# Hybrid encoder block on one core: source order for the first stage's ScalarE and VectorE, and a last norm through rows of sums, a root and a reciprocal

## Chip, cores and metric

The kernel runs on one core of a Trainium2 chip. The metric is the device time of one execution in microseconds (us), the median of several runs.

## What is computed

One encoder layer for two token streams (512 prompt tokens, 1024 sample tokens, width 1024, all float32): a norm, one input projection, differential attention beside a recurrent branch (RG-LRU), an output projection with residual, a second norm, a SwiGLU FFN with residual, and a final norm.

```python
def rmsnorm(x, g):
    xf = x.astype(jnp.float32)
    y = xf * lax.rsqrt(jnp.mean(xf * xf, axis=-1, keepdims=True) + NORM_EPS)
    return (y * g.astype(jnp.float32)).astype(x.dtype)

def encoder_layer(x, ...):
    h = rmsnorm(x, norm_mix)
    q, k, v, xr, gate = jnp.split(h @ w_in, [...], axis=-1)
    ...
    x = x + jnp.concatenate([o, y_lru], axis=-1) @ w_out
    h2 = rmsnorm(x, norm_ffn)
    return x + (jax.nn.silu(h2 @ w_gate) * (h2 @ w_up)) @ w_down
...
    return rmsnorm(x, norm_final)
```

The two places that the change touches are the first `rmsnorm` with the first columns of `h @ w_in` for the prompt, and the final `rmsnorm` for the prompt's last 256 tokens.

## The kernel before, in words

Tokens are held in three blocks of 512 (block 0 the prompt, 1 and 2 the sample), features on the 128 partitions, so a block is eight chunks of 128 x 512. A float32 operand is split into a high part `h` (a rounding to float32r, a cast on ScalarE) and a low part `l` (the rest, a subtraction on VectorE), and every product is three matmuls, h·h, l·h and h·l (`mm3`, L213 to L215).

The instructions are not queued as the source lists them: the tile framework sets the order on each engine from its own estimate of when operands come, and every engine then runs its list strictly in order. Side work (attention, the recurrence, loading the next block) is recorded beside the projection by `advance`, a table of numbers (A1, A2, ...) saying how much of it per step.

The first stage (L856 to L863). `load_block(0, ...)` (L290 on) asks for the block's four pages `xc` (512 KB each, L314) on SyncE's DMA queue, and between the first page and the others for the first weight tile (`fetch(1)`, L191 to L202: DMA `wr`, cast `wh` L200, subtraction `wl` L201). Per chunk it makes `xh` (ScalarE, scaled by the norm's gain, L326) and `xl` (VectorE, L327). The norm's factor is one number per token; it is worked out beside the projection: the squares of the eight chunks (L307, added up by L309), sums over partitions by TensorE (`ss`, L279), a Newton root in twelve small VectorE instructions (L281, L248 to L253), diagonal matrices `dg` (L261) which TensorE turns into a row spread over all partitions (`bc`, L262), and a ScalarE copy of it, `rms` (L339). A projected tile is evicted by multiplying it with that row (`ev`, L375). The projection has three PSUM banks (`pm`), so a fourth tile can't start before the first tile's `ev`. `constants()` (L146) follows: ScalarE makes four scaled copies of each half of a distance table (`d`, L152, from the load L149), which go to DRAM (L153); `lv` and a chain of small VectorE instructions (`tmp`) make scalars that attention needs. Attention of the prompt's first head loads its keys, values (`vr`) and queries back from DRAM, transposes the values on TensorE (`pt`, L514) and makes scores (`sc`, L582 and L583).

The end (L1190 on). The FFN's second product for the prompt's upper output half runs in two token halves, T0 and T1; `finish(0, T0)` (L1094) runs beside T1's matmuls, and after the last matmul come, with nothing beside them: the residual adds (L1079), squares (L1088) and their sum (L1090), the same norm chain for 256 tokens (L279, L281, L248 to L253, L261, L262), a copy of the row (L1103, for GpSimd, which scales two of the eight chunks), the scaling (L1109), and four output DMAs.

Of the kernel before, what the change touches and what calls it, by code (L numbers as in the profile page):

```python
# [11 lines left out]
F32 = mybir.dt.float32  # L12
F32R = mybir.dt.float32r
I32 = mybir.dt.int32
F16 = mybir.dt.float16
AF = mybir.ActivationFunctionType
# [4 lines left out]
P = 128  # L21
D = 1024
KC = D // P
# [7 lines left out]
EPS = 1e-6  # L31
LAM_INIT = 0.2
HALF = (P, BLK)
# [14 lines left out]
YV, YF, YL, YT = 1.0, 1.5, 3.0, 1.5  # L48
GRP, LB, FINE = 1, 5, 4
# [27 lines left out]
def drain(gen):  # L77
    for _ in gen:
        pass


def build(tc, io, es):
    nc = tc.nc
    V, A, T = nc.vector, nc.scalar, nc.tensor
# [4 lines left out]
    cp = pool(es, "const")  # L89
# [3 lines left out]
    rings = {}  # L93
# [17 lines left out]
    def bank(name, tag):  # L111
        return banks[tag].tile([P, BLK], F32, name=name, tag=tag)
# [15 lines left out]
    onesq = cp.tile([P, P], F32, name="onesq")  # L128
# [2 lines left out]

    warm = cp.tile([P, 1], F32, name="warm")
    A.activation(warm, ones, AF.Exp)
    neglam = cp.tile([P, 1], F32, name="neglam")
    subg = cp.tile([P, 1], F32, name="subg")
    hb = cp.tile([P, 16], F32, name="hb")
# [3 lines left out]
    def split(h, l, src, eng=V):  # L140
        A.copy(h, src)  # L141
        eng.tensor_tensor(l, src, h.bitcast(F32), ALU.subtract)  # L142
# [46 lines left out]


    plan, ahead = [], []  # L191

    def fetch(n):
        while plan and len(ahead) < n:
            key = plan.pop(0)
            r = rings["raw"]([P, KC, P], "wr")
            nc.sync.dma_start(r, io[key[0]][key[1]].rearrange("p (k m) -> p k m", k=KC))
            h = rings["w"]([P, KC, P], "wh", F32R)
            l = rings["w"]([P, KC, P], "wl", F32R)
            A.copy(h, r)  # L200
            V.tensor_tensor(l, r, h.bitcast(F32), ALU.subtract)  # L201
            ahead.append((key, (h, l)))  # L202
# [53 lines left out]
    def bcast_cols(tag, r, c0, who="m", n=4):  # L256

        bc = bank("bc", tag)
        for i in range(n):
            dg = small(P, "dg")  # L260
            V.tensor_scalar(dg, ident, r[:, c0 + i:c0 + i + 1], None, ALU.mult)  # L261
            T.matmul(bc[:, i * P:(i + 1) * P], lhsT=onesq, rhs=dg, start=True, stop=True)  # L262
        return bc[:, 0:n * P]
# [11 lines left out]
    def inv_rms_cols(tag, acc, n=4):  # L275

        ss = bank("ss", tag)
        for i in range(n):
            T.matmul(ss[:, i:i + 1], lhsT=acc[:, i * P:(i + 1) * P], rhs=ones, start=True, stop=True)  # L279
        ve = small(n, f"ve{n}")  # L280
        V.tensor_scalar(ve, ss[:, 0:n], 1.0 / D, EPS, ALU.mult, ALU.add)  # L281
        return rsqrt_cols(ve, n)
# [15 lines left out]
    def load_block(b, other=None, xring="raw"):  # L298

        h, l = acts[b] = Block(f"xh{b}", F32R), Block(f"xl{b}", F32R)  # L300
        acc = rings["mh"](HALF, "sqa")
        pages = []

        def square(c):
            r = pages[c // 2][:, c % 2]
            sq = rings["mh"](HALF, "sq") if c else acc
            A.activation(sq, r, AF.Square)  # L307
            if c:
                V.tensor_tensor(acc, acc, sq, ALU.add)  # L309

        def load():
            i = len(pages)
            pages.append(rings[xring]([P, 2, BLK], "xc"))
            nc.sync.dma_start(pages[i], chunks(io["xt"][b], 2 * i))  # L314

        for c in range(KC):
            if c == 0 and other is not None:
                for i in range(4):
                    load()
                    if i == 0:  # L320
                        other()
            elif c % 2 == 0 and other is None:
                load()
            r = pages[c // 2][:, c % 2]
            g = par[:, C_MIX + c:C_MIX + c + 1]
            A.activation(h[c], r, AF.Copy, scale=g)  # L326
            V.scalar_tensor_tensor(l[c], r, g, h[c].bitcast(F32), ALU.mult, ALU.subtract)  # L327
            if b:
                square(c)
            yield 2.0  # L330
        if b == 0:
            for c in range(KC):
                square(c)
        r = inv_rms_cols("lru", acc)
        if b:
            yield YL
        bc = bcast_cols("lru", r, 0)
        rows[b] = rings["rows"](HALF, f"rms{b}")
        A.copy(rows[b], bc)  # L339
        yield 2.0  # L340
# [7 lines left out]
    IN_P = qkv_tiles(0, 1, 2, 3) + lru_tiles(0, 1, 2, 3)  # L348
    IN_S = sum((lru_tiles(i - 4) if i > 3 else qkv_tiles(i) for i in ORDER), [])

    def proj(s, blocks, tiles, ready):

        first = len(blocks) + GRP
        n = len(blocks) * BLK
        xr = None
        for t0 in [0] + list(range(first, len(tiles))):
            group = tiles[t0:t0 + (1 if t0 else first)]
            w, dst = {}, {}
            for m in group:
                w[m] = load_w("w_in", m)  # L360
                if m >= 16:
                    dst[m] = gt = rings["lru"]([P, n], "gt")
                elif m >= 12:
                    xr = rings["xr"]([P, SEQ_S + 32], f"xr{s}")
                    V.memset(xr[:, 0:2], 0.0)
                    V.memset(xr[:, n + 2:n + 3], 0.0)
                    dst[m] = xr[:, 2:n + 2]

            def scaled(pm, m, b):
                o = slice(b * BLK, (b + 1) * BLK)  # L370
                if m in dst:
                    V.tensor_tensor(dst[m][:, o], pm, rows[blocks[b]], ALU.mult)
                else:
                    ev = rings["mh"](HALF, "ev")
                    V.tensor_tensor(ev, pm, rows[blocks[b]], ALU.mult)  # L375
                    nc.scalar.dma_start(qkv[s][m][:, o], ev)

            late = []
            for b, blk in enumerate(blocks):
                for m in group:  # L380
                    pm = bank("pm", "mm")
                    dense(pm, w[m], acts[blk])
                    if blk in rows:
                        scaled(pm, m, b)
                    else:
                        late.append((pm, m, b))
                    yield 5.1
            for args in late:
                scaled(*args)
            done[s].update(group)  # L390
            if group[-1] >= 16:
                ready.append((group[-1] - 16, xr, gt))
# [402 lines left out]
    ALL, T0, T1 = slice(0, BLK), slice(0, BLK // 2), slice(BLK // 2, BLK)  # L795
# [25 lines left out]
    ready = {"p": [], "s": []}  # L821
# [12 lines left out]
    n = (B1 + B2 + 3 + GRP) // 2  # L834
# [18 lines left out]
    for _ in range(WARM):  # L853
        T.matmul(spare[:, 0:P], lhsT=onesq, rhs=onesq, start=True, stop=True)

    lb = load_block(0, lambda: fetch(1), "main")  # L856
    for _ in range(KC):
        next(lb)
    p = proj("p", [0], IN_P, ready["p"])
    for _ in range(1 + GRP):  # L860
        next(p)
    drain(lb)
    constants()  # L863
    advance(p, 92.0, (att_p, A1, 0.0, 1.0), (scan, A2, 0.6, 1.0), (load_block(1), 20.0, A3, 1.0))

    lb = load_block(2)
    for _ in range(LB):
        next(lb)
    p = proj("s", [1, 2], IN_S, ready["s"])
# [14 lines left out]
    bc = inv_rms("pv", sums)  # L884
# [129 lines left out]
    def x_chunk(b, m, tok):  # L1014
        return xs[b][m // 2][:, m % 2, tok]
# [59 lines left out]
    def add(b, ms, acc, tok=ALL, square=False, last=False):  # L1075

        for m, a in zip(ms, acc):
            y = x_chunk(b, m, tok)
            V.scalar_tensor_tensor(y, a, 0.5, y, ALU.mult, ALU.add)  # L1079
            if square:  # L1080
                add_square(b, m, tok)
            if last and m in POOLED:
                A.mul(y, y, par[:, C_FIN + m:C_FIN + m + 1])

    def add_square(b, m, tok):
        key = b, tok.start
        sq = rings["xh" if key in sums else "sums"](HALF, "sqd")[:, 0:tok.stop - tok.start]
        A.activation(sq, x_chunk(b, m, tok), AF.Square)  # L1088
        if key in sums:
            V.tensor_tensor(sums[key], sums[key], sq, ALU.add)  # L1090
        else:
            sums[key] = sq

    def finish(b, tok, tag, last=False):  # L1094

        n = (tok.stop - tok.start) // P
        r = inv_rms_cols(tag, sums[b, tok.start], n)
        yield YF
        bc = bcast_cols(tag, r, 0, n=n)
        yield 1.0  # L1100
        if last:
            row = rings["xh"](HALF, "bcs")[:, tok]
            A.copy(row, bc)  # L1103
        for c in range(KC):
            y = x_chunk(b, c, tok)
            if last and c in POOLED:
                nc.gpsimd.tensor_tensor(y, y, row, ALU.mult)
            else:
                V.scalar_tensor_tensor(y, y, par[:, C_FIN + c:C_FIN + c + 1], bc, ALU.mult, ALU.mult)  # L1109
            if c % 2:  # L1110
                (nc.sync if c % 4 == 1 else nc.scalar).dma_start(chunks(io["out"][b], c - 1)[:, :, tok], xs[b][c // 2][:, :, tok])
            yield 1.0
# [121 lines left out]
```

## Time and profile before

| what | value |
|---|---|
| median of 3 runs | 1765.14 us (1763.05 to 1765.33) |
| the profiled execution's own time | 1766.5 us |
| its span, first to last instruction | 1764.6 us |
| TensorE busy, its mean granted clock | 98% of the span, 0.993 |
| VectorE, ScalarE, GpSimd busy | 75%, 47%, 0% |

The span is what the trace's rows lie in; 1.9 us of the profiled execution are outside it. Busy time of TensorE is modelled (a matmul's row is longer than the distance to the next one), so what is read from it is where it stood idle, and for whom. Rows give the start from the span's start and a duration in us; "L213" is a line of the kernel.

### The profile page before, as it was taken

How to read it: one execution, taken by the hardware profiler on the slowest of the kernel's cores; microseconds unless marked ns; L12 is line 12 of the kernel's file. 1: busy time of each engine (PE TensorE's matmuls, PEld its weight loads, DVE VectorE, ACT ScalarE, POOL GpSimd, SP SyncE). 2: the span in 40 equal slices, each digit the busy share in tenths (PEclk: the TensorE clock that was granted, in tenths of full speed). 3: DMA queues.
4: the chain of work that ended last, by engine and by line, in shares of the span. 5: the costliest groups of instructions: out<-in, count | busy, mean ns of one | idle time of the engine just before them, and what ended most of it. 6: DMA issues, size and time to landing. Idle time of an engine off the chain costs nothing.

```text
span 1764.6 us, 22706 instructions
## 1 busy us (share of the span) xinstructions
PE 1731.0 (98%) x8316; PEld 1432.0 (81%) x8316; DVE 1317.0 (75%) x2291; ACT 830.7 (47%) x1327; POOL 1.6 (0%) x6
## 2 busy tenths in 40 slices
PE   8998999999999999999999989999999999999997
PEld 7787877878878888888878878888888888888897
DVE  6779878778678777787453897777777777987784
ACT  6568657664455554555342443332223334445451
POOL 0000000000000000000000000000000000000000
PEclk9999999999999999999999999999999999999998
DMA  8532423244383322221364643222323229743261
GB/s 295 185 122 95 155 90 127 71 156 155 103 231 119 114 72 96 84 84 66 125 227 125 191 152 111 101 101 92 107 104 123 92 88 321 264 127 98 96 198 54
DMA packets 103870, 234.56 MB, mean 133 GB/s; under 512 B 12112, under 2 KB 21072, under 8 KB 103760
## 3 DMA queue, kind: packets, MB, share of 16 engines
q1 hardware_dynamic: 75456, 180.85, 32.4%
q10 hardware_dynamic: 28304, 52.28, 7.8%
q8 instruction: 65, 1.06, 0.3%
q14 instruction: 45, 0.37, 0.1%
HBM read 175.80 MB, written 57.28 MB: 132 GB/s over the span
## 4 chain that ended last, share of the span: by engine, by line
PE 88%; DVE 5%; ACT 3%; DMA 3%; issue 1%; SPq 0%; DVEq 0%; ACTq 0%
PE pm L213 5%; PE pm L214 5%; PE pm L215 5%; PE gu L213 4%; PE gu L215 4%; PE gu L214 4%; PE acc L213 4%; PE acc L215 4%; PE acc L214 4%; PE y L213 3%; PE y L215 3%; PE y L214 3%; PE z L215 2%; PE z L213 2%; PE z L214 2%; PE x L215 2%
## 5 line engine op out<-in xcount | busy, mean ns | idle before, releaser
L213 PE MATMUL pm<-xh,wh 128*128 128x512 f32 x480 | 191.0, 398 | 6.0 <-ACT wh L200 3.3
L214 PE MATMUL pm<-xl,wh 128*128 128x512 f32 x480 | 190.0, 396 | 0.8 <-DVE xl L327 0.8
L215 PE MATMUL pm<-xh,wl 128*128 128x512 f32 x480 | 189.7, 396 | 0.0
L200 ACT CAST wh<-wr 128x1024 fp32r<-128x1024 f32 x100 | 105.1, 1051 | 148.5 <-PE gu L214 61.2
L213 PE MATMUL gu<-yh,wh 128*128 128x512 f32 x352 | 142.0, 403 | 0.9 <-DVE ev L375 0.9
L213 PE MATMUL acc<-hp,ws 128*128 128x512 f32 (+1 forms) x396 | 140.5, 355 | 0.0
L215 PE MATMUL acc<-hp,ws 128*128 128x512 f32 (+1 forms) x396 | 140.3, 354 | 0.0
L214 PE MATMUL acc<-hp,ws 128*128 128x512 f32 (+1 forms) x396 | 140.1, 354 | 0.0
L215 PE MATMUL gu<-yh,wl 128*128 128x512 f32 x352 | 139.0, 395 | 0.0
L214 PE MATMUL gu<-yl,wh 128*128 128x512 f32 x352 | 138.6, 394 | 0.0
L201 DVE TENSOR_TENSOR wl<-wr,wh 128x1024 fp32r<-128x1024 f32 x100 | 122.2, 1222 | 17.5 <-ACT wh L200 16.7
L588 ACT ACTIVATE pb<-pb,mn 128x1024 f32<-128x1024 f32 (+1 forms) x96 | 97.0, 1010 | 73.9 <-DVE mn L585 73.8
L585 DVE CUSTOM_DVE_ANT_0 pb<-sc,tab 128x1024 f32<-128x1024 f32 (+1 forms) x96 | 100.1, 1043 | 34.2 <-PE sc L583 32.9
L710 ACT CAST ws<-s 128x512 fp32r<-128x512 f32 x88 | 54.8, 624 | 126.2 <-PE x L215 47.5
L213 PEld LDWEIGHTS pm<-xh,wh 128*128 128x128 f32 x480 | 91.3, 190 | 24.6 <-ACT wh L200 3.5
L214 PEld LDWEIGHTS pm<-xl,wh 128*128 128x128 f32 x480 | 91.3, 190 | 19.4 <-DVE xl L327 1.1
L215 PEld LDWEIGHTS pm<-xh,wl 128*128 128x128 f32 x480 | 91.0, 190 | 19.1 <-DVE wl L201 0.7
L141 ACT CAST hp<-hr 128x512 fp32r<-128x512 f32 (+1 forms) x143 | 77.8, 552 | 56.2 <-PE acc L215 24.4
L142 DVE TENSOR_TENSOR hp<-hr,hp 128x512 fp32r<-128x512 f32 (+1 forms) x143 | 85.3, 608 | 24.8 <-ACT hp L141 21.3
L710 ACT CAST ws<-wr 128x512 fp32r<-128x512 f32 x66 | 41.2, 624 | 102.5 <-PE z L215 43.8
L215 PEld LDWEIGHTS acc<-hp,ws 128*128 128x128 f32 x396 | 74.9, 189 | 10.4
L213 PEld LDWEIGHTS acc<-hp,ws 128*128 128x128 f32 x396 | 74.9, 189 | 10.3
(269 smaller groups left out, 4301.2 us busy)
## 6 DMA issues: line engine op xcount, KB each, us to landing
wr<-w_gate SPq DMA_DIRECT2D x44, 512.0 KB, 3.5
wr<-w_up SPq DMA_DIRECT2D x44, 512.0 KB, 3.5
wr<-w_in SPq DMA_DIRECT2D x40, 512.0 KB, 4.1
hr<-hs SPq DMA_DIRECT2D x77, 256.0 KB, 2.7
hs<-t ACTq DMA_DIRECT2D x44, 256.0 KB, 2.0
hs<-ht ACTq DMA_DIRECT2D x33, 256.0 KB, 2.9
wr<-w_out SPq DMA_DIRECT2D x16, 512.0 KB, 3.6
xc<-xt SPq DMA_DIRECT2D x12, 512.0 KB, 4.0
```

What stands on the lines that cost most here:

```text
L141: A.copy(h, src)
L142: eng.tensor_tensor(l, src, h.bitcast(F32), ALU.subtract)
L200: A.copy(h, r)
L201: V.tensor_tensor(l, r, h.bitcast(F32), ALU.subtract)
L213: T.matmul(out, lhsT=wh, rhs=ah, start=first, stop=False, skip_group_check=more)
L214: T.matmul(out, lhsT=wh, rhs=al, start=False, stop=False, skip_group_check=more)
L215: T.matmul(out, lhsT=wl, rhs=ah, start=False, stop=last, skip_group_check=more)
L585: V.tensor_tensor_reduce(out=pp[m], in0=sc, in1=tab[:, 896 - q0:896 - q0 + n], scale=-0.125, scalar=3e38, op0=ALU.add, op1=ALU.min, accum_ ...
L588: A.activation(pp[m], pp[m], AF.Exp, scale=-1.0, bias=mn, accum_out=zz)
L710: A.copy(h[:, 0], src)
```

## The change

Two places. In the first stage ScalarE and VectorE keep the order of the source (`manual_schedule`), which is rewritten: the first weight tile is loaded and split in two halves that alternate with the first pages and chunks, the second weight is fetched behind the chunks, then four squares, the third weight, four squares. In the last norm (`finish(..., last=True)`) the squares of the last two chunks are not added to the sum: TensorE takes the sum and the two squares as right operands under a matrix of ones, which gives the sum already as a row in all partitions; ScalarE takes the root, VectorE the reciprocal, and ScalarE copies it. A dummy root in the norm of T0 brings the table of the root in ahead.

```diff
+    eps = cp.tile([P, 1], F32, name="eps")
+    V.memset(eps, EPS)
...
+    def first_halves():
+        key = plan.pop(0)
+        r = rings["raw"]([P, KC, P], "wr")
+        h = rings["w"]([P, KC, P], "wh", F32R)
+        l = rings["w"]([P, KC, P], "wl", F32R)
+        src = io[key[0]][key[1]].rearrange("p (k m) -> p k m", k=KC)
+        halves = [slice(0, KC // 2), slice(KC // 2, KC)]
+        for o in halves:
+            nc.sync.dma_start(r[:, o], src[:, o])
+            yield
+        for o in halves:
+            split(h[:, o], l[:, o], r[:, o])
+            yield
+        ahead.append((key, (h, l)))
+        yield
...
                 for i in range(4):
                     load()
-                    if i == 0:
-                        other()
-            elif c % 2 == 0 and other is None:
+                    if i < 2:
+                        next(other)
+            elif c in (1, 2, 3) and other is not None:
+                next(other)
+            if c % 2 == 0 and other is None:
                 load()
...
             for c in range(KC):
                 square(c)
+                if c == 3:
+                    yield 0.0
...
-    lb = load_block(0, lambda: fetch(1), "main")
-    for _ in range(KC):
+    p = proj("p", [0], IN_P, ready["p"])
+    with tc.manual_schedule(engines={mybir.EngineType.Activation, mybir.EngineType.DVE}):
+        lb = load_block(0, first_halves(), "main")
+        for _ in range(KC):
+            next(lb)
+
+        fetch(2)
         next(lb)
-    p = proj("p", [0], IN_P, ready["p"])
-    for _ in range(1 + GRP):
-        next(p)
-    drain(lb)
+        fetch(3)
+        drain(lb)
+        for _ in range(1 + GRP):
+            next(p)
     constants()
...
             if square:
-                add_square(b, m, tok)
+                add_square(b, m, tok, last and m >= KC - 2)
+        for m in ms:
             if last and m in POOLED:
+                y = x_chunk(b, m, tok)
                 A.mul(y, y, par[:, C_FIN + m:C_FIN + m + 1])
...
+        if apart:
+            sq = rings["xh"](HALF, "sqd")[:, 0:tok.stop - tok.start]
+            A.activation(sq, x_chunk(b, m, tok), AF.Square)
+            if not isinstance(sums[key], list):
+                sums[key] = [sums[key]]
+            sums[key].append(sq)
+            return
...
+        w = tok.stop - tok.start
+        if last:
+            ss, bc = bank("ss", tag)[:, 0:w], bank("rb", tag)[:, 0:w]
+            for k, a in enumerate(sums[b, tok.start]):
+                T.matmul(ss, lhsT=onesq, rhs=a, start=k == 0, stop=k == len(sums[b, tok.start]) - 1)
+            root = rings["xh"](HALF, "root")[:, 0:w]
+            A.activation(root, ss, AF.Sqrt, scale=1.0 / D, bias=eps)
+            V.reciprocal(bc, root)
+            row = rings["xh"](HALF, "bcs")[:, 0:w]
+            A.copy(row, bc)
+        else:
+            r = inv_rms_cols(tag, sums[b, tok.start], w // P)
+            if tok is T0:
+                A.activation(warm, r[:, 0:1], AF.Sqrt)
+            yield YF
+            bc = bcast_cols(tag, r, 0, n=w // P)
```

The order moves on every engine. First, ScalarE at the start of the program; before, from its first square to the second weight:

```order
L307 ACTIVATE sqa<-xc 128x512
L307 ACTIVATE sq<-xc 128x512
L200 CAST wh<-wr 128x1024
L326 ACTIVATE xh_292<-xc,par 128x512 x2
L326 ACTIVATE xh_293<-xc,par 128x512 x2
L326 ACTIVATE xh_294<-xc,par 128x512 x2
L326 ACTIVATE xh_295<-xc,par 128x512 x2
L200 CAST wh<-wr 128x1024
L307 ACTIVATE sq<-xc 128x512 x2
```

and now (VectorE's `xl` and `wl` stand in the same order):

```order
L347 ACTIVATE xh_296<-xc,par 128x512
L143 CAST wh<-wr 128x512
L347 ACTIVATE xh_296<-xc,par 128x512
L143 CAST wh<-wr 128x512
L347 ACTIVATE xh_297<-xc,par 128x512 x2
L347 ACTIVATE xh_298<-xc,par 128x512 x2
L347 ACTIVATE xh_299<-xc,par 128x512 x2
L219 CAST wh<-wr 128x1024
L326 ACTIVATE sqa<-xc 128x512
L326 ACTIVATE sq<-xc 128x512 x3
```

The two squares ahead of the first cast are gone, and the first weight's casts stand as halves between the first chunks.

Second, ScalarE around the copy of the norm's row, `rms`; before (`gh` is the recurrence's gate weight, `xh` by now the next block's):

```order
L152 ACTIVATE d_467<-d_456 128x960
L200 CAST wh<-wr 128x1024
L326 ACTIVATE xh_558<-xc,par 128x512 x2
L141 CAST gh<-gr 128x512
L200 CAST wh<-wr 128x1024
L339 COPY rms_454<-bc 128x512
L152 ACTIVATE d_472<-d_470 128x960
L152 ACTIVATE d_475<-d_470 128x960
```

and now:

```order
L154 ACTIVATE d_481<-d_470 128x960
L347 ACTIVATE xh_566<-xc,par 128x512 x2
L143 CAST gh<-gr 128x512
L154 ACTIVATE d_486<-d_484 128x960
L154 ACTIVATE d_489<-d_484 128x960
L362 COPY rms_405<-bc 128x512
L219 CAST wh<-wr 128x1024
L154 ACTIVATE d_492<-d_484 128x960
```

Two pieces of the distance table's second half (`d_486`, `d_489`) now stand ahead of the row's copy, and a weight's cast, the fourth weight's, right behind it. On VectorE the first `ev` stands behind that weight's `wl`, as it stood behind a later weight's before.

Third, TensorE at the transposes of the first head's values, `pt`; before:

```order
L213 MATMUL pm<-xh_293,wh 128x512
L214 MATMUL pm<-xl_297,wh 128x512
L514 MATMUL pt<-ident,vr 128x128 x4
L215 MATMUL pm<-xh_293,wl 128x512
L213 MATMUL pm<-xh_294,wh 128x512
```

and now:

```order
L232 MATMUL pm<-xh_299,wh 128x512
L233 MATMUL pm<-xl_303,wh 128x512
L537 MATMUL pt<-ident,vr 128x128 x4
L234 MATMUL pm<-xh_299,wl 128x512
L232 MATMUL pm<-xh_299,wh 128x512
```

Counted from the first matmul of the fourth tile, 59 matmuls stood ahead of `pt` before and 44 do now.

## Rows read from the trace of the kernel before

**Rows 1.** The page, busy time by engine, whole span.

```profile
PE 1731.0 (98%) x8316; PEld 1432.0 (81%) x8316; DVE 1317.0 (75%) x2291; ACT 830.7 (47%) x1327; POOL 1.6 (0%) x6
```

**Rows 2.** The timeline of TensorE: start, us, what, and idle time before, by releaser.

```profile
29.96 0.50 PE L213 MATMUL pm<-xh,wh 128*128 128x512 f32 x1 [1.40 <-DVE ev L375]
...
46.90 0.50 PE L582 MATMUL sc<-kt,qh 128*128 128x512 f32 x1 [1.17 <-ACT qh L141]
...
48.91 0.80 PE L583 MATMUL sc<-kt,ql 128*128 128x512 f32 x1 [0.81 <-DVE ql L142]
...
175.51 0.80 PE L213 MATMUL pm<-xh,wh 128*128 128x512 f32 x1 [3.27 <-ACT wh L200]
```

**Rows 3.** Windows: busy by engine in a stretch, PEclk, DMA share, GB/s.

```profile
30.00:45.70 15.70, 15.70 (x70) 12.65 (x70) 9.30 (x34) 7.33 (x12) 0.00 (x0) 1.00 0.93 297
...
48.90:52.30 3.40, 3.39 (x8) 2.72 (x9) 1.97 (x4) 1.75 (x3) 0.00 (x0) 0.52 0.41 164
...
178.00:180.00 2.00, 2.00 (x6) 1.61 (x5) 1.97 (x2) 2.00 (x4) 0.00 (x0) 0.50 0.75 240
```

**Rows 4.** The timelines of ScalarE and VectorE, first 15 us.

```profile
6.10 1.05 ACT L200 CAST wh<-wr 128x1024 fp32r<-128x1024 f32 x1 [0.23 <-DMA wr<-w_in]
7.05 5.02 ACT L326 ACTIVATE xh<-xc,par 128x512 fp32r<-128x512 f32 x8
...
8.32 5.38 DVE L327 SCALAR_TENSOR_TENSOR xl<-xc,par,xh 128x512 fp32r<-128x512 f32 x8
13.62 1.22 DVE L201 TENSOR_TENSOR wl<-wr,wh 128x1024 fp32r<-128x1024 f32 x1
```

**Rows 5.** DMA issues at 17.40, 22.61 and 38.86 us: KB, us to landing.

```profile
xc<-xt SPq DMA_DIRECT2D x1, 512.0 KB, 3.6
...
d<-dist SPq DMA_DIRECT2D x1, 480.0 KB, 5.7
...
vr<-qkvp SPq DMA_DIRECT2D x1, 256.0 KB, 4.4
```

**Rows 6.** The timelines of TensorE, VectorE and ScalarE, 18 to 34 us.

```profile
18.55 3.67 ACT L152 ACTIVATE d<-d 128x960 f16<-128x960 f32 x4
...
22.51 0.16 DVE L281 TENSOR_SCALAR ve<-ss 128x4 f32<-128x4 f32 x1 [1.21 <-PE ss L279]
...
27.84 0.71 PE L262 MATMUL bc<-dg,onesq 128*128 128x128 f32 x4 [0.28 <-DVE dg L261]
...
28.59 0.59 ACT L339 COPY rms<-bc 128x512 f32<-128x512 f32 x1 [1.05 <-PE bc L262]
...
29.21 1.89 DVE L375 TENSOR_TENSOR ev<-pm,rms 128x512 f32<-128x512 f32 x3
...
33.22 0.33 ACTq L376 DMA_DIRECT2D qkvp<-ev  x1
```

**Rows 7.** The timeline of the last norm, all engines, from its last sums on.

```profile
1751.76 1.47 DVE L1090 TENSOR_TENSOR sqd<-sqd 128x256 f32<-128x256 f32 x3
...
1753.94 0.16 DVE L281 TENSOR_SCALAR ve<-ss 128x2 f32<-128x2 f32 x1 [0.70 <-PE ss L279]
...
1756.73 1.20 PE L262 MATMUL bc<-dg,onesq 128*128 128x128 f32 x4 [2.83 <-DVE dg L261]
1757.96 0.37 ACT L1103 COPY bcs<-bc 128x256 f32<-128x256 f32 x1 [5.67 <-PE bc L262]
```

**Rows 8.** VectorE's groups by shape: busy us, mean ns of one, idle before.

```profile
L523 DVE RECIPROCAL cf<-z 128x1 f32<-128x1 f32 x48 | 7.7, 161 | 16.6 <-ACT pb L588 16.4
L1090 DVE TENSOR_TENSOR sqd<-sqd 128x256 f32<-128x256 f32 x14 | 5.7, 420 | 1.0 <-ACT sqd L1088 0.8
...
L176 DVE RECIPROCAL tmp<-tmp 128x8 f32<-128x8 f32 x1 | 0.2, 202 | 0.0
```

**Rows 9.** The timeline of ScalarE: a table load, and the longest gap beside T1's matmuls.

```profile
1.67 1.28 ACT L133 ACT_TABLE_LOAD   x1 [1.67 <-PEq L1226]
...
1734.20 0.41 ACT L141 CAST hp<-hr 128x256 fp32r<-128x256 f32 x1 [6.64 <-PE acc L215]
```

More of the change, by code (lines that the diff above doesn't have):

```diff
@@ L1080, in add, with add_square @@
             if square:
-                add_square(b, m, tok)
+                add_square(b, m, tok, last and m >= KC - 2)
+        for m in ms:
             if last and m in POOLED:
+                y = x_chunk(b, m, tok)
                 A.mul(y, y, par[:, C_FIN + m:C_FIN + m + 1])
-    def add_square(b, m, tok):
+    def add_square(b, m, tok, apart=False):
         key = b, tok.start
+        if apart:
[5 more added lines that the diff above has]
+            return
         sq = rings["xh" if key in sums else "sums"](HALF, "sqd")[:, 0:tok.stop - tok.start]
@@ L1094, in finish @@
     def finish(b, tok, tag, last=False):
[L1096 to L1099, printed above, removed]
+        w = tok.stop - tok.start
[14 more added lines that the diff above has]
+            bc = bcast_cols(tag, r, 0, n=w // P)
         yield 1.0
-        if last:
-            row = rings["xh"](HALF, "bcs")[:, tok]
-            A.copy(row, bc)
         for c in range(KC):
```

## The prediction

> **What bounds the kernel now.** I read the page's busy line first: TensorE is busy 98% of the span [rows 1]. So only time in which TensorE stands idle, or runs at a lower clock, can be won or lost. TensorE's timeline of the first 60 us shows where that is near the change: 1.40 us at 29.96, for the first eviction `ev`, and 1.17 and 0.81 us at 46.90 and 48.91, for the query's parts `qh` and `ql` [rows 2]. The windows then show what a wait costs beyond itself: at full clock 70 matmuls take 15.70 us, 0.224 us each, while from 48.90 to 52.30, behind the two waits, the granted clock was 0.52, the lower of its two levels (1.2 against 2.4 GHz); 3.40 us there are 1.7 us lost [rows 3]. The other place is the end: after the last add of residuals a chain runs with nothing beside it, and every us of it is a us of the kernel [rows 7].
>
> The profiled execution took 1766.5 us, 1.36 above the median 1765.14. The sum below is made against 1766.5, and its difference is then applied to the median.
>
> **The end.** Before, three adds run from 1751.76 to 1753.23 (1.47), the sums `ss` and their hand-over take 0.70 to 1753.94, the root, `dg` and `bc` run to 1757.93 (1756.73 + 1.20), 3.99 in all, and the copy `bcs` follows at once [rows 7]. Part by part:
>
> - Two adds go. One of this size is 0.42 [rows 8], so the sum is ready at 1752.18 instead of 1753.23: **-1.05**. The two squares that take their place are ScalarE's as before.
> - `ss` becomes three float32 matmuls with 256 columns instead of one-column ones. Their price is not in the trace; nearest is `bc`, a pair with 128 columns each: 0.71 in one row [rows 6] and 1.20 at the end [rows 7], after an idle 2.83. If the 0.49 between them is a clock of one half, a pair is 0.49 of columns and 0.22 of fixed time at full clock. Six such pieces of 128 columns are three pairs: 3 x 0.49 + 0.22 = 1.69, or 3.16 at the lower clock. I take 1.69, since TensorE has been idle well under 1 us when `ss` starts; against 0.70 that is **+1.0** (bound: +2.5).
> - The chain of 3.99 goes: **-3.99**.
> - A root of 128x256 out of PSUM on ScalarE: as the copy of the same shape there, 0.37 [rows 7], and 0.08 of hand-over: **+0.45**.
> - A reciprocal of 128x256. The trace has two: one element per partition is 161 ns, eight are 202 ns [rows 8], so 5.9 ns an element, and 161 + 255 x 5.86 ns = **+1.65**. If it is as cheap as an add of that shape it is 0.42 [rows 8]; that is the lower bound. Both are rows of the same engine; I take the one of the same operation.
>
> The sum is -1.94, **-2.0** with rounding: the copy `bcs` starts near 1756.3 instead of 1757.96. With the cheap reciprocal it is -3.2, with `ss` at the lower clock -0.5. The scaling and the four output DMAs behind it stay. The table for the root is loaded in T0's norm: a load is 1.28, and ScalarE has a gap of 6.64 beside T1's matmuls [rows 9], so it costs nothing; without that cover it would add 1.28 to the end.
>
> A rule speaks against the reciprocal. The Trainium skill ("VectorE: DVE Perf Modes", section "First, the fixed hardware budget") says that the engine divides iteratively, with a repeat count of 8. Taken as eight passes over 256 elements at the 0.96 GHz that it gives for the engine, my estimate from that page is 2.1 us; by it the end would be -1.5. The measured slope of 5.9 ns an element lies between one pass and eight, so it stays the basis.
>
> **The start: first chunks.** The first weight's cast began when its 512 KB had landed (6.10), `xh` ran from 7.05 and the last `xl` ended at 13.70 [rows 4]. With halves the first `xh` need not wait for the cast, and two squares that stood ahead of it are gone; two casts of half a tile cost no more than one but for a fixed part. Bounds: no gain (the loads decide), or the 0.95 between 6.10 and 7.05, which `xh` stood behind the cast. I take 0.85, so the first three tiles of TensorE end 0.85 sooner, near 27.7 instead of 28.56 (29.96 less 1.40 [rows 2]). That is not kept: the fourth tile waits for the first `ev`.
>
> **The start: the norm's row.** The sums `ve` came at 22.51 [rows 6]; with the chunks 0.9 sooner and VectorE's work unchanged, they come at 21.1 to 21.6. A `wl` of 1.22 [rows 4] that stood in the middle of the root now stands behind, so `bc`, done at 28.55 (27.84 + 0.71), is done at 25.9 to 26.4. But ScalarE's copy `rms` now stands behind `d_486` and `d_489`, which need the table's second half. Its load sits on SyncE's queue behind the write of `d_475`; the first half's four pieces ended at 22.22 (18.55 + 3.67 [rows 6]), each 0.92, so `d_475` ends half of that sooner and the load can go at 20.3 instead of 22.61 [rows 5]. It lands 3.6 later (as the page `xc` at 17.40) or 5.7 later (as this load did before, amid others) [rows 5]: 24.0 to 26.0. Then two `d` (1.85), the copy (0.59), the fourth weight's cast (1.05) and `wl` (1.22) and one `ev` (0.63, a third of 1.89 [rows 6]): 5.34, and some 0.3 of hand-overs, so TensorE goes on at **29.65 to 31.6** against 29.96. I take 29.7, since `xc` is the load nearest in time, and `bc` would allow no more than that. TensorE then idles some 2.0 there instead of 1.40.
>
> **The start: values and queries.** What follows `ev` is partly earlier: the third tile's write to DRAM stood behind all four pieces `d` (33.22 [rows 6]), now behind two and casts, near 31. Values `vr` were issued at 38.86 and landed at 43.26 (4.4 [rows 5]); by the write alone 41.1, by the evictions alone 43.0. But `pt` has moved ahead: 44 matmuls x 0.224 after 29.7 is 39.6, where before 59 made 43.2, just when `vr` was there. So a **new wait** for `vr` stands at 39.6: 1.5 to 3.4, taken 2.2. What is queued behind it on TensorE is the projection itself. In return the waits for `qh` and `ql` (1.17 + 0.81 [rows 2]) go: the chain of scalars that stood ahead of them on VectorE starts from the load `lv`, which SyncE now sends ahead of two of the table's writes instead of behind all. Waiting is then 2.0 + 2.2 instead of 1.40 + 1.98; with restart 0.3 sooner and 0.85 of head start spent, TensorE's path gains 0.3 at 29.7, loses 2.2 at 39.6 and wins 2.0 back near 47. The half-clock stretch of 1.7 may come after either wait, as it did after 1.98 us of waits in two pieces; the wait of 3.27 at 175.51 was followed by a granted clock of 0.50 too [rows 2, 3], that of 1.40 by 1.00. I keep it at one such stretch: **0** for the whole start (-2 to +4). The middle of the program has the same order as before.
>
> **Sum.** -2.0 at the end, 0 at the start: 1764.5 for the profiled execution, and 1765.14 - 2.0 = **1763.2** for the median. A measurement of this kernel tells 0.2%, 3.5 us, from no change.
>
> **The rivals.**
>
> *The start wins* (0.22): the waits at 29.7 and 39.6 stay short, no stretch runs at half clock (-1.7), and the reciprocal is nearer an add (-3.2 at the end). For it: 1.40 at 29.96 left the clock at 1.00. Against it: the rows of the table and `pt` both moved to earlier than their loads. Time: 1765.14 - 3.2 - 1.7 = 1760.3, and less where both waits shrink.
>
> *The table's second half comes late* (0.12), the slower side. The load lands 5.7 or more after its issue, at 26 or after; copy, cast and `ev` follow, TensorE restarts at 31.6 (+1.6) and has idled 4, more than the 3.27 which was followed by a clock of 0.50 from 178 to 180 at least [rows 2, 3]. If that drop lasts 6.8 us, double the 3.4 us of the earlier stretch, it costs 3.4. With only 1.5 won at the end: 1765.14 + 1.6 + 3.4 - 1.5 = 1768.6. It decides from a landing at about 26; below that the row's own chain is the later one. For it: this same load took 5.7 [rows 5]; the DMA share was 0.93 from 30 on [rows 3]. Against: at 20.3 the queue ahead is shorter.
>
> *The sums run at the lower clock* (0.15): `ss` takes 3.16, the end gives 0.5, and the time is 1764.6, no change. For it: `bc` at the end took 1.20 [rows 7]; against it: that came after 2.83 of idle time. The skill's slow reciprocal would end in the same band, at 1763.6.
>
> *The change does not do what it says*: the order printed ahead shows that it does, on all three engines, so no chance is kept for it.
>
> **Numbers.** My forecast (0.51) and the sums at the lower clock lie within 0.2%; of the start's win two thirds goes beyond it, as does some of my own range (-2 at the start with -2 at the end): faster 0.23. The late table gives slower 0.12, with a little from the +4 of the start. The range runs from 1759.9 (the start's win with a little more) to 1767.4 (forecast with +4, or the late table in part).
>
> **What would show it.** Right, if in the profile after: VectorE has a RECIPROCAL 128x256 of about 1.65; `bcs` starts near 4.1 after the first add's end (before 5.8); the last `xl` ends near 12.8; `ve` near 21.3 and the second load of the table lands at 24; TensorE waits 2.0 for `ev` until 29.7, then some 2.2 for `vr` near 39.6, and no longer for `qh`, `ql`; a table load stands in ScalarE's gap beside T1. Wrong, if the reciprocal is over 2.5 or under 0.8, if `ss` takes 3, if TensorE restarts after 31, or if windows from 30 to 60 us show more than one stretch, or none, near 0.5.

## The result and the profile after

The changed kernel takes 1777.01 us (median of 6 runs, 1775.86 to 1780.26) against 1765.24 before: 11.8 us slower, ratio 1.0067 (95% interval 1.0057 to 1.0077). The forecast was 1763.2, the range ended at 1767.4. The profiled execution took 1777.2 us, its span is 1775.4.

The page's busy line, which answers to [rows 1]:

```profile
PE 1744.4 (98%) x8314; PEld 1430.2 (81%) x8314; DVE 1316.2 (74%) x2278; ACT 830.6 (47%) x1331; POOL 1.6 (0%) x6
```

TensorE has two rows fewer and is busy 13.4 us longer. So most of the time did not go into a new wait. The view of TensorE's waits says the same; its first rows, before (line, releaser, us in total, times, the longest):

```profile
PE y L213 <- ACT ws L710: 4.7, 1, 4.7
PE bc L262 <- DVE dg L261: 4.2, 7, 2.8
PE pm L213 <- ACT wh L200: 3.3, 1, 3.3
PE ss L279 <- DVE sqd L1090: 1.9, 1, 1.9
PE pm L213 <- DVE ev L375: 1.4, 1, 1.4
```

and after:

```profile
PE y L232 <- ACT ws L733: 4.7, 1, 4.7
PE pm L232 <- ACT wh L219: 3.3, 1, 3.3
PE pm L232 <- DVE ev L398: 3.0, 1, 3.0
PE bc L281 <- DVE dg L280: 1.6, 6, 0.5
```

Added up, the rows of this view give 26.1 us before and 21.1 after: TensorE waits 5 us less, and the program's span is 10.8 us longer.

Where it falls behind is found by setting the same matmul of the two timelines side by side. The start of some of them in us, each taken from TensorE's timeline (`pr` is a product of the recurrence's gates, `po` of the output projection; `x`, `y` and `z` are sums of the FFN's gate and up products for the sample, `acc` of its second product):

```
matmul                       before     after   difference
first score sc                46.90     45.02      -1.88
first pr                     113.17    112.13      -1.03
first po                     352.66    353.06      +0.40
po, second half begins       916.72    917.54      +0.82
last po                      981.78    984.51      +2.73
first x                     1046.46   1048.97      +2.52
last x                      1461.58   1470.91      +9.33
last acc                    1751.11   1763.77     +12.66
```

The start is a little ahead. Then the loss grows in steps, most of it in the second half of `po` and in the FFN (from `x` on), over stretches in which TensorE hardly ever waits. The windows count it: before,

```profile
700.00:800.00 100.00, 99.78 (x540) 83.63 (x539) 73.95 (x134) 51.00 (x83) 0.00 (x0) 1.00 0.24 80
905.00:955.00 50.00, 49.78 (x219) 41.03 (x219) 17.93 (x23) 11.23 (x15) 0.00 (x0) 1.00 0.47 146
1100.00:1400.00 300.00, 300.00 (x1325) 248.39 (x1325) 225.53 (x346) 92.57 (x157) 0.00 (x0) 1.00 0.29 101
1520.00:1600.00 80.00, 80.00 (x355) 66.24 (x354) 68.22 (x112) 34.48 (x61) 0.00 (x0) 1.00 0.43 129
```

and after:

```profile
700.00:800.00 100.00, 99.78 (x538) 83.47 (x537) 73.62 (x133) 51.05 (x84) 0.00 (x0) 1.00 0.23 78
905.00:955.00 50.00, 49.48 (x211) 39.67 (x212) 18.18 (x23) 11.71 (x16) 0.00 (x0) 1.00 0.47 146
1100.00:1400.00 300.00, 300.00 (x1305) 244.74 (x1304) 221.82 (x341) 92.37 (x158) 0.00 (x0) 1.00 0.29 101
1520.00:1600.00 80.00, 80.00 (x349) 65.18 (x348) 69.63 (x115) 34.56 (x61) 0.00 (x0) 1.00 0.50 161
```

From 1100 to 1400 us TensorE is busy all the time, at a granted clock of 1.00 in both, the DMA share is the same, and 1305 matmuls go through instead of 1325. On average each takes 1.5% longer. Which ones, the groups by tile of that stretch tell (count, busy us, mean ns of a row). A tile like `b1512h` is the high part of chunks that enter the FFN's products as the moving operand (called chunks b1 below); `ws` holds the weights. In the kernel before every group there has a mean of 389, two of them:

```profile
L213 PE MATMUL y<-b6512h,ws 128*128 128x512 f32 x64 | 24.9, 389 | 0.0
...
L213 PE MATMUL x<-b0512h,ws 128*128 128x512 f32 x64 | 24.9, 389 | 0.0
```

After:

```profile
L232 PE MATMUL x<-b1512h,ws 128*128 128x512 f32 x64 | 25.3, 396 | 0.0
L232 PE MATMUL y<-b6512h,ws 128*128 128x512 f32 x64 | 25.3, 396 | 0.0
L232 PE MATMUL z<-b4512h,ws 128*128 128x512 f32 x64 | 25.1, 392 | 0.0
...
L232 PE MATMUL y<-b5512h,ws 128*128 128x512 f32 x62 | 24.3, 391 | 0.0
...
L232 PE MATMUL x<-b0512h,ws 128*128 128x512 f32 x60 | 23.8, 396 | 0.0
...
L232 PE MATMUL y<-b3512h,ws 128*128 128x512 f32 x61 | 23.7, 389 | 0.0
...
L232 PE MATMUL z<-b2512h,ws 128*128 128x512 f32 x60 | 23.3, 389 | 0.0
```

The same instruction on the same shapes: chunks b0, b1 and b6 as moving operand are slow, b2 and b3 are not, b4 and b5 lie a little above them. What these chunks differ in is not in the profile but in the built program, which lists the address of every tile (bytes in a partition):

```
tile                            before    after   after, modulo 256
ws (weights, one of x's)        106496   106528     32
b0512h                          225024   225024      0
b1512h                          216832   216832      0
b6512h                          192256   192256      0
b2512h                           36864    65568     32
b3512h                           32768    32800     32
```

Before, all six are at 0 modulo 256. (b2 also lies in another slot of its ring now.)

The program places its tiles in on-chip memory from both ends. The left side holds the constants, a spacer named `edge_left` and then the rings of weights and the main operands; the right side has a spacer `edge` and the rings of attention, recurrence and FFN. The change puts a new constant, `eps`, on the left side; it occupies 32 bytes of each partition and **moves everything behind it on the left side by 32 bytes**, the weights and main operands from multiples of 256 to 32 beyond them. The right side stays. Slow are the matmuls whose moving operand is on the right and whose weights are on the left; where both are on the left, both have moved alike.

The end, which answers to [rows 7], did what was forecast:

```profile
1764.43 0.42 DVE L1128 TENSOR_TENSOR sqd<-sqd 128x256 f32<-128x256 f32 x1
...
1764.90 1.56 PE L1139 MATMUL ss<-sqd,onesq 128*128 128x256 f32 x6 [0.85 <-DVE sqd L1128]
...
1766.50 0.47 ACT L1141 ACTIVATE root<-ss,eps 128x256 f32<-128x256 f32 x1 [1.54 <-PE ss L1139]
...
1767.01 1.76 DVE L1142 RECIPROCAL rb<-root 128x256 f32<-128x256 f32 x1 [2.16 <-ACT root L1141]
...
1768.80 0.37 ACT L1144 COPY bcs<-rb 128x256 f32<-128x256 f32 x1 [1.83 <-DVE rb L1142]
```

From the start of the last FFN matmul to the end of the span it was 13.5 us (1764.6 - 1751.11) and is now 11.6 (1775.4 - 1763.77). The root's table is loaded in ScalarE's gap, at 1740.41, 24 us ahead of the chain.

The start, which answers to [rows 2, 4, 5, 6]:

```profile
8.16 0.62 ACT L143 CAST wh<-wr 128x512 fp32r<-128x512 f32 x1 [0.76 <-DMA wr<-w_in]
...
9.43 4.07 DVE L348 SCALAR_TENSOR_TENSOR xl<-xc,par,xh 128x512 fp32r<-128x512 f32 x6
...
20.72 0.43 SPq L151 DMA_DIRECT2D d<-dist  x1
...
22.20 0.17 DVE L300 TENSOR_SCALAR ve<-ss 128x4 f32<-128x4 f32 x1 [1.21 <-PE ss L298]
...
25.90 1.90 ACT L154 ACTIVATE d<-d 128x960 f16<-128x960 f32 x2 [2.05 <-DMA d<-dist]
27.71 0.57 ACT L362 COPY rms<-bc 128x512 f32<-128x512 f32 x1
28.17 1.04 ACT L219 CAST wh<-wr 128x1024 fp32r<-128x1024 f32 x1
...
29.25 1.23 DVE L220 TENSOR_TENSOR wl<-wr,wh 128x1024 fp32r<-128x1024 f32 x1 [1.99 <-ACT wh L219]
30.39 1.88 DVE L398 TENSOR_TENSOR ev<-pm,rms 128x512 f32<-128x512 f32 x3
...
31.22 0.47 PE L232 MATMUL pm<-xh,wh 128*128 128x512 f32 x1 [3.05 <-DVE ev L398]
```

### The profile page after: what moved, and what is told of

Same layout as the page of the kernel before. It is cut to its first block, busy times and chain, and to the rows that moved or that the text cites. A ratio compares the mean times of both kernels' runs of the same rounds, so it can differ in the third digit from the quotient of the medians.

```text
span 1775.4 us, 22695 instructions
## 1 busy us (share of the span) xinstructions
PE 1744.4 (98%) x8314; PEld 1430.2 (81%) x8314; DVE 1316.2 (74%) x2278; ACT 830.6 (47%) x1331; POOL 1.6 (0%) x6
## 4 chain that ended last, share of the span: by engine, by line
PE 88%; DVE 5%; ACT 4%; DMA 2%; issue 1%; SPq 0%; DVEq 0%; ACTq 0%
PE pm L232 5%; PE pm L233 5%; PE pm L234 5%; PE gu L232 5%; PE gu L234 5%; PE gu L233 4%; PE acc L232 4%; PE acc L233 4%; PE acc L234 4%; PE y L232 3%; PE y L233 3%; PE y L234 3%; PE x L233 2%; PE x L232 2%; PE z L232 2%; PE x L234 2%
```

## Experiments

**Theory A**: the 32 bytes. A matmul slows down when the addresses of its moving operand and of weights (its own, or the next matmul's, which are loaded beside it: before, those of the matmul at 9.46 us from 9.22 on, beside the one at 9.12) don't agree modulo some power of two. **Theory B**: the new order of instructions, at the start or in the last norm, slows the matmuls. All kernels run beside the kernel before; each time is given with the before of the same runs.

### The shift alone, and the change without it

The kernel before, with the spacer 32 bytes longer in each partition (8 columns of 4 bytes):

```diff
-    pool(es, "edge_left").tile([P, 32], F32, name="edge_left")
+    pool(es, "edge_left").tile([P, 40], F32, name="edge_left")
```

> The kernel before, with not one instruction changed: the unused tile edge_left is 32 bytes a partition longer, so that all tiles of the left side start where they start in the changed kernel (20512 instead of 20480), and those of the right side stay. Theory A (the address: matmuls whose moving operand lies on the right side and whose weights lie on the left take 233.5 instead of 226.7 ns when the two stand 32 bytes apart modulo 64): the changed kernel's loss between 113 us and the last matmul, 1.0 + 12.7 = 13.7 us, comes back here: 1779 us, po 233 ns a matmul. Theory B (the order of instructions at the start or in the last norm slows the matmuls): no change, 1765 us, po 227 ns.

Measured: 1778.39 us against 1765.8, ratio 1.0075 (1.0057 to 1.0092).

The changed kernel, with the spacer 32 bytes shorter:

```diff
-    pool(es, "edge_left").tile([P, 32], F32, name="edge_left")
+    pool(es, "edge_left").tile([P, 24], F32, name="edge_left")
```

> The changed kernel, with not one instruction changed: the unused tile edge_left is 32 bytes a partition shorter, which makes up for the new tile eps; the left side starts at 20480 again. Theory A: 1777.0 - 13.7 = 1763.3 us, that is the start's gain of 1.0 and the last norm's 1.9 alone, 1762.3; between 1762 and 1764. Theory B: no change against the changed kernel, 1777 us.

Measured: 1764.91 against 1765.8, ratio 0.9999 (0.9988 to 1.0010). A spacer that nobody reads makes the whole loss, and takes it away: theory B has fallen. The groups of the same stretch (least, median and greatest ns of a row), first of the kernel before with the shift:

```profile
L214 PE MATMUL x<-b0512l,ws x64: 395/396/397, 1099.7 to 1391.8; 128*128 128x512 f32 x64
```

then of the changed kernel without it:

```profile
L232 PE MATMUL x<-b0512h,ws x64: 389/389/389, 1109.7 to 1397.4; 128*128 128x512 f32 x64
```

The second came out 0.9 us above the range that was expected: the shift is worth 1777.01 - 1764.91 = 12.1 us (12.7 if each is taken against its own before), less than the 13.7 read off one profiled execution, and the rest of the change is worth less than the 2.9 read there: 0.9, with an interval that includes none.

### What must agree, and modulo what

Both in the kernel before: the left side moved by 64 and by 128 bytes (`edge_left` 48 and 64 columns).

> The kernel before with the left side 64 bytes further (20544). Theory A with a period of 64 bytes: 1765 us, no change. Theory A with a longer period (128 bytes or the whole of a page): slower by some 14 us, as with 32. Theory B: no change.

Measured: 1776.07 against 1765.8, ratio 1.0057 (1.0041 to 1.0074). So not 64.

> The kernel before with the left side 128 bytes up. Theory A with a period of 256 bytes (or more): slower like the shifts by 32 and 64, 1776 us, x 232 to 233 ns a matmul (the matmuls po whose operands stand 128 apart in the kernel before took 232). Theory A with a period of 128 bytes: no change, 1765.5 us.

Measured: 1776.64 against 1765.72, ratio 1.0062 (1.0048 to 1.0075). So not 128 either.

Both sides moved, the left by 32 bytes up and the right by 32 down (`edge` from 56 to 64 columns):

> The kernel before with both sides moved by 32 bytes (left up, right down), so that moving operands and weights stand at 32 modulo 64 alike. Theory A, relative (what counts is that the two differ): 1765 us, no change. Theory A, absolute (what counts is that an operand stands off a multiple of 64): at least as slow as with the left side alone, 1779 us or more, with pm and gu slow too. Theory B: no change.

Measured: 1776.11 against 1765.8, ratio 1.0064 (1.0044 to 1.0083). That fits neither line: it is slower, but not with pm and gu slow too (start to start 228.8 and 229.5 ns on average, against 228.5 and 229.2 before). The two sides then stand 64 bytes apart, and with 64 not neutral the run does not tell relative from absolute. The next one does: the right side down by 224 (`edge` 112 columns), so that both stand at 32 modulo 256.

> The kernel before with the left side 32 bytes up and the right side 224 bytes down, so that both stand at 32 modulo 256; in the earlier run with 32 and -32 the two sides stood 64 apart and the kernel was 0.6% slower. Theory A relative (the moving operand and the weights that are loaded beside it must agree modulo 256): no change, 1765.5 us, x and y 226.7 ns a matmul. Theory A absolute (an operand off a multiple of 256 is slow): 1777 us or more, x 233 ns.

Measured: 1767.22 against 1765.72, ratio 1.0011 (1.0002 to 1.0020). Relative, then: every moving operand and every weight of these products is off a multiple of 256, and the cost is gone but for 1.5 us, which stay unexplained (its x is at 389, and between the two profiled executions the matmuls of 512 columns add up to the same within 0.2 us). The groups of left by 64, left by 128 and both alike:

```profile
L214 PE MATMUL x<-b1512l,ws x63: 393/394/398, 1099.7 to 1389.9; 128*128 128x512 f32 x63
```

```profile
L213 PE MATMUL x<-b1512h,ws x64: 392/394/398, 1101.4 to 1391.8; 128*128 128x512 f32 x64
```

```profile
L213 PE MATMUL x<-b1512h,ws x64: 389/389/389, 1100.2 to 1386.8; 128*128 128x512 f32 x64
```

The changed kernel and the same kernel with the shorter spacer run the same matmuls in the same order, so each can be set beside itself. The time from its start to the next start, of the matmuls of 512 columns (those without a wait behind them, under 270 ns), by addresses modulo 256 in the changed kernel:

```
moving operand agrees with      count   changed, ns   short spacer, ns   sum, us
its own weights and the next's   4120      228.5           227.8          +2.9
its own, not the next's           353      232.4           231.4          +0.4
neither                          1809      233.4           227.3         +11.0
the next's, not its own             1      235             228             0.0
```

The sums make 14.3 us; these two profiled executions are 13.9 us apart, since other matmuls and waits give 0.4 back. The loss is in the matmuls that disagree with both. Those that disagree with the next's weights alone are slow in both kernels and differ by 1 ns, and only one disagrees with its own alone: which of the two weights counts is not shown. Nor is why 4120 matmuls that agree with both take 0.7 ns more. In pure runs of one tile a distance is 226.7 ns (x before) and 233.4 (x after).

### The same rule at another place

The kernel before itself had such matmuls. Its tile `xr` is 1056 columns wide, 4224 bytes, so that tiles behind it on the right side stood 128 bytes off, those of the first `po` among them:

```profile
L213 PE MATMUL po<-ih,wh x61: 387/392/404, 352.7 to 401.4; 128*128 128x512 f32 x61
```

```diff
-                    xr = rings["xr"]([P, SEQ_S + 32], f"xr{s}")
+                    xr = rings["xr"]([P, SEQ_S + 64], f"xr{s}")
```

In the changed kernel with `edge_left` at 24 columns:

> The changed kernel with the left side back at 20480 and one tile of the right side, xr, 32 columns (128 bytes) wider, so that every tile behind it on the right side starts at a multiple of 256 too. Theory A with a period of 256 bytes: in the kernel before some 360 matmuls of 512 columns, a third of po among them, had a partner 128 bytes off and took 231 to 234 instead of 227 ns; they come down to 227, 1.9 us in all, so 1.9 us below the changed kernel with the left side back (1764.9 beside a before of 1765.8): 1763.0 us. If those matmuls are slow for another reason: no change, 1764.9 us, and that third of po stays at 232 ns.

Measured: 1762.55 against 1765.03, ratio 0.9986 (0.9977 to 0.9995); in the kernel before alone:

> The kernel before with the tile xr 128 bytes wider and nothing else, so that all operands on the right side stand at multiples of 256 bytes: the same step as in the changed kernel, where it gave 1.6 to 2.4 us. Theory A: 1.9 us below before, 1763.3 us, all of po at 227 ns.

Measured: 1764.2 against 1765.57, ratio 0.9990 (0.9981 to 0.9999). In the first of the two, 191 such matmuls fall from 232.6 to 227.8 ns from start to start, beside the same kernel without the wider `xr`; that is 0.9 us, where the times say 1.6. Its first `po`, and that of the second:

```profile
L232 PE MATMUL po<-ih,wh x64: 387/389/396, 351.8 to 401.9; 128*128 128x512 f32 x64
...
L213 PE MATMUL po<-ih,wh x64: 388/389/397, 351.3 to 401.4; 128*128 128x512 f32 x64
```

The rule told a gain at a place that the change doesn't touch, though both intervals end close to no change. The changed kernel with both sides at multiples of 256 has the lowest median of all.

### The end and the start, each alone

The kernel before with the new last norm alone (`edge_left` at 24 columns, so that `eps` moves nothing):

> The kernel before with the new last norm alone; edge_left is 32 bytes shorter, so that the new tile eps moves no other tile. If the terms of the last norm add up as in the changed kernel's trace, the span from the last matmul of the FFN to the end falls from 13.5 to 11.6 us and nothing else moves: 1765.5 - 1.9 = 1763.6 us. If the new norm also slows matmuls (theory B): 1776 us.

Measured: 1764.38 against 1765.72, ratio 0.9993 (0.9984 to 1.0002): 1.3 us less, though the interval includes no change. The kernel before with the new first stage alone:

> The kernel before with the new first stage alone, no new tile, so no address moves. If the start keeps what it was ahead at 100 us in the changed kernel: 1.0 us less, 1764.5 us. If later waits take that back: 1765.5 us. If the new order at the start is what slows the matmuls (theory B): 1776 us.

Measured: 1766.19 against 1765.72, ratio 1.0003 (0.9994 to 1.0012): no change. That one execution is 1.0 us ahead at 100 us says little: the kernel with the new end alone, whose start is that of before, was 0.97 ahead at the first `pr` too.

Two runs asked what holds the start back. First, in the changed kernel with `edge_left` at 24 columns, the tables behind the evictions (`constants()` inside the part that keeps its order, the scalars in a function of their own behind it):

> The changed kernel with the left side back at 20480, and the eight pieces of the distance table written behind the first evictions in the order that ScalarE keeps, the scalars' load behind them in the source; so the copy of the norm's row no longer waits for the table's second half (5.1 us from issue to landing in the changed kernel, TensorE idle for 3.05 us and then at half clock for 3.4 us). If that wait is what holds the start back, TensorE restarts by 29 us, with under 1.5 us of idle time there and no half clock right behind: 1.5 to 3 us below the changed kernel with the left side back, 1762 to 1763.4 us. If what follows waits instead (keys, values, queries or the table for the first scores), the gain is given back: 1765 us or more.

Measured: 1769.38 against 1765.03, ratio 1.0020 (1.0011 to 1.0029): slower than before, as the last line of the expectation has it. Its timeline at the row's copy, the eviction and the values:

```profile
27.78 0.59 ACT L364 COPY rms<-bc 128x512 f32<-128x512 f32 x1 [5.18 <-PE bc L283]
...
31.32 0.77 PE L234 MATMUL pm<-xh,wh 128*128 128x512 f32 x1 [3.33 <-DVE ev L400]
...
52.62 0.63 PE L539 MATMUL pt<-ident,vr 128*128 128x128 f32 x4 [1.06 <-DMA vr<-qkvp]
```

The copy comes no sooner without the table, at 27.78 against 27.71: there it waits for `bc`, whose chain had two `xl` of the next block between its steps. In the changed kernel `bc` ended at 27.24, so the table held the copy back by under 0.5 us. And the attention's inputs are late in turn: `pt` starts at 52.62, in the changed kernel at 42.95.

Then, on top of the fastest kernel, the fourth weight split behind the second four squares (one more `yield` in `load_block` and a `fetch(4)` behind it):

> The changed kernel with both sides at multiples of 256 bytes, and the fourth weight asked for and split behind the second four squares, so that its cast and its subtraction (some 2.1 us on the way from the row's copy to the first eviction) stand ahead of the root. If those two hold the start back, more than the distance table, whose move behind the evictions left TensorE waiting 3.3 us for them all the same: TensorE restarts by 30 us with an idle of 1.5 us or less and no half clock right behind, 1 to 2.5 us below the changed kernel with both sides aligned (2.5 below before): 3.5 to 5 us below before, 1760 to 1761.5 us. If a later wait (values at pt) takes it back: 2.5 us below before, 1762.5 us.

Measured: 1765.2 against 1765.57, ratio 0.9996 (0.9987 to 1.0005).

```profile
29.81 0.50 PE L232 MATMUL pm<-xh,wh 128*128 128x512 f32 x1 [2.31 <-DVE ev L398]
45.64 1.09 PE L537 MATMUL pt<-ident,vr 128*128 128x128 f32 x4 [2.39 <-DMA ld<-qkvp]
```

TensorE restarts 1.4 us sooner than in the changed kernel and then waits 2.39 where `pt` stands: given back, in the direction of the second line of the expectation and further: 0.4 us below before, not 2.5. The row names `ld`, but `pt` reads the values: their load left at 40.15 and took 5.4 us to land, just before 45.64 (in the changed kernel 39.23 and 3.3).

## Why the prediction was wrong

**The step that failed** is the one sentence "The middle of the program has the same order as before", taken as a cost of nothing. The sentence is true, and the conclusion false. `eps` stands in no term of the sum, and its 32 bytes moved weights against the moving operands that stayed: 1809 matmuls took 233.4 ns instead of 227.3, 11.0 us, and 4473 others 3.3 us more; in the times the shift alone is worth 12.1 us, more than the whole loss of 11.8. None of the rivals was this. The late table, slower by the forecast too, is another mechanism and did not make the loss. The chance of 0.12 for slower rested on it and, a little, on the start's +4.

**The end** was right in the trace, term by term: `ss` 1.56 (1.69 forecast, at full clock), root 0.47 (0.45), reciprocal 1.76 (1.65), the table hidden, -1.9 for -2.0. Its time alone, 1.3 us less, is not clear of no change. The slope of two small reciprocals was the better guide. By the Trainium skill ("VectorE: DVE Perf Modes", section "First, the fixed hardware budget") the estimate was 2.1 for eight passes; the row has 1.76, so the rule gives the direction (far over an add's 0.42) and overstates the size here.

**The start's sum** of 0 held (+0.5 alone, inside its interval), its steps less so. The last `xl` ended at 13.50, not 12.85, because the weight's second half landed only at 8.16; `ve` came at 22.20, not 21.1 to 21.6. The table's second half landed at 25.9, near the late end of 24.0 to 26.0, where I had taken the early one, and TensorE went on at 31.22, not 29.7, past the 31 that was named as a sign of being wrong. The table was not all that was late: the row itself, `bc`, was done at 27.24, not 25.9 to 26.4, and with the table out of the way the copy began no sooner. The wait of 2.2 for `vr` at 39.6 did not show, since TensorE came later; without the shift it is 0.80 at 42.85. The waits for `qh` and `ql` are gone (0.3 left), and one stretch at half clock stayed one, now behind the 3.05 us: the granted clock is 0.50 from 32.0 to 35.2.

**What was not tried**: why two addresses that differ modulo 256 cost 6 to 7 ns in a matmul of 512 columns, whether it is the matmul's own weights or the next's, and whether it holds for other types. The 0.7 ns of the matmuls that agree and the remaining 1.5 us of the run with both sides alike are open.

## What to carry to other kernels

A new tile, however small, moves those behind it: with each edit set the built program's list of addresses beside the old one, and keep moving operands and weights of such products (float32r, 512 columns) equal modulo 256 bytes. When a kernel that TensorE bounds gets slower and its waits do not grow, group its matmuls by tile and read the mean of each group, at a window without waits. That an order is unchanged is no reason for a cost of nothing; the same groups in the trace of before already showed 392 against 389.

## What the hardware showed that was not expected

Distances from start to start of float32r matmuls of 512 columns at full clock, by how far the weights start above the moving operand modulo 256: 226.7 ns at 0 (x before), 233.4 at 32 (x after), 233.3 at 64 (x with the left side 64 up) and 232.8 at 128 (x with the left side 128 up). The direction matters: with the moving operand 64 above the weights, the first `po` with the left side 64 up takes 229.3. For 256 columns no such loss was seen: 259 matmuls of the changed kernel whose weights stand 32 above take 119.9 ns, and 121.5 in the same kernel with the short spacer.
